# Transposing the values in 32x32 blocks on VectorE and placing the blocks through DRAM

## The chip, the cores and the metric

One core of a Trainium2 chip runs the kernel. It has a matrix engine (TensorE, PE in the profile), a vector engine (VectorE, DVE), an activation engine (ScalarE, ACT), a general engine (GpSimd, POOL) and a sync engine (SyncE, SP), which here issues all DMAs. The metric is the device time of one execution in microseconds; lower is better.

## The reference

The kernel computes one decoder layer on x (1024 tokens by 1024 channels, fp32). After an RMS norm one projection gives eight parts. Three mixers work beside each other: causal pooling, stick-breaking attention with 8 heads of 64 channels, and softmax attention to 256 memory tokens. Every result is multiplied by SiLU of its gate, and an output projection and the residual follow. The part around the change is the stick-breaking attention, cut to what matters:

```python
h = rmsnorm(x, norm_g)
proj = h @ w_in        # pool_v|pool_gate|sb_q|sb_k|sb_v|sb_gate|mem_q|mem_gate
z = (q @ k.T) * Dh**-0.5                       # per head, strictly causal
log_beta, log_1m_beta = log_sigmoid(z), where(mask, log_sigmoid(-z), 0)
cum = cumsum(log_1m_beta, axis=-1)
a = where(mask, exp(log_beta + cum[..., -1:] - cum), 0)
y_sb = (a @ v) * silu(gate)
```

## The kernel before

Matrix products are made in two parts. Each fp32 operand is split into a rounded high part and the rest, its low part, and three products are added up in PSUM (`hh` times `wh`, `hl` times `wh`, `hh` times `wl`).

**Units.** A projection of 128 channels is a `Unit`: two halves of 512 tokens, each of eight steps of three matmuls (L218, L221), and after each half's last step an `evac` function that takes the result out of PSUM. The result stands with the channel on the partition and the token along the row. While a unit starts, the weights of the next one are loaded (L149, on SP), rounded by ACT (L160) and subtracted by POOL (L164).

**The value unit.** For a pair of heads p there is a query, a key, a value and a gate unit. The stick-breaking sum is rewritten by parts, so that the attention multiplies not by v but by the difference between neighbouring tokens. `evac` in `v_unit` makes it: ACT copies the half into `vt` one column to the right (L307), POOL puts the last column of the half before (or a zero, L304) into column 0 (L306), and DVE subtracts (L310). `vt` has one buffer. The attention needs these values with the token on the partition, so a later step, `late`, turns them: PE transposes four blocks of 128x128 into one PSUM bank (L318), ACT rounds them to the high part (L321), and DVE subtracts for the low part (L322). Both go to V, where each head of each block of 128 tokens has 64 columns of high and 64 of low parts.

**Order.** The order of PE's instructions is written by hand. `chain` strings the steps of units together. It puts the first `late` of a value unit at step 13 of that same unit and the second at step 5 of the next unit. `weave` mixes such a string of filling steps into the steps of an attention (first the memory attention, then the four head pairs in turn), by costs that the steps carry (0.43 us for `late`). After the opening stage the order on DVE, ACT, POOL and SP is laid out when the kernel is built, by a planner that takes an instruction once its inputs should be there; on the chip each engine then runs its list in that order. The values of pairs 0 and 1 are made beside the memory attention, those of pairs 2 and 3 beside the attentions of pairs 1 and 2.

Of the kernel before, what the change touches and what calls it, by code (L numbers as in the profile page):

```python
# [8 lines left out]
F32 = mybir.dt.float32  # L9
F32R = mybir.dt.float32r  # L10
AF = mybir.ActivationFunctionType
ALU = mybir.AluOpType
AX = mybir.AxisListType

P = 128
S = 1024
# [4 lines left out]
HD = 64  # L21
# [4 lines left out]
def layer_kernel(  # L26
# [15 lines left out]
    nc = tc.nc  # L42
    const = ctx.enter_context(tc.tile_pool(name="const", bufs=1))
    pool = ctx.enter_context(tc.tile_pool(name="pool", bufs=1))
    psum = ctx.enter_context(tc.tile_pool(name="psum", bufs=1, space=bass.MemoryType.PSUM))

    xv = x[0]
# [5 lines left out]
    def f(ap):  # L53
        return ap.bitcast(F32)
# [3 lines left out]
    def ps(tag, name):  # L58
        return psum.tile([P, 512], F32, tag=tag, name=name, bufs=banks[tag])
# [7 lines left out]
    bufs = {"wr": 1, "wh": 2, "wl": 2, "be": 4}  # L67
# [4 lines left out]
    def slot2(tag, name, dt=F32):  # L72
        return pool.tile([P, 2048], dt, tag=tag, name=name)
# [9 lines left out]
    ident = const.tile([P, P], F32, name="ident")  # L83
# [155 lines left out]
    def chain(units, after=None):  # L239
        steps, rest = [], []  # L240
        for n, u in enumerate(units):
            nxt = units[n + 1] if n + 1 < len(units) else after
            a = list(u.steps)
            if nxt is not None:
                a[0] = (KC, lambda f0=a[0][1], nxt=nxt: (f0(), nxt.weights()))
            if u.late is not None:
                a = a[:13] + u.late(0) + a[13:]
            steps += a[:5] + rest + a[5:]
            rest = u.late(1) if u.late is not None else []
        return steps + rest  # L250

    def lazy(make):
        box = []

        def get():
            if not box:
                box.append(make())
            return box[0]

        return get  # L260
# [35 lines left out]

    def v_unit(e0, name, tag):
        get = lazy(lambda: slot2(tag, f"V_{name}", dt=F32R)[:].rearrange("p (t h c) -> p t h c", t=NT, h=2))
        box = {}

        def evac(th, c, pt):
            vt = pool.tile([P, 513], F32, tag="vt", name=f"vt_{name}_{th}", bufs=1)
            if th == 0:
                nc.gpsimd.memset(vt[:, 0:1], 0.0)  # L304
            else:
                nc.gpsimd.tensor_copy(vt[:, 0:1], vlast[:])  # L306
            nc.scalar.activation(vt[:, 1:513], pt[:], AF.Copy)  # L307
            if th == 0:
                nc.gpsimd.tensor_copy(vlast[:], vt[:, 512:513])
            nc.vector.tensor_tensor(vt[:, 0:512], vt[:, 0:512], pt[:], op=ALU.subtract)  # L310
            box[th] = vt

        def late(th):
            def fn():
                v, vt = get(), box[th]
                tp = ps("tr", f"tv_{name}_{th}")
                for i in range(4):
                    nc.tensor.transpose(tp[:, i * P : (i + 1) * P], vt[:, i * P : (i + 1) * P], ident[:])  # L318
                b = slice(4 * th, 4 * th + 4)
                tpv = tp[:].rearrange("p (b h c) -> p b h c", b=4, h=2)  # L320
                nc.scalar.activation(v[:, b, :, 0:HD], tpv, AF.Copy)  # L321
                nc.vector.tensor_tensor(v[:, b, :, HD:P], tpv, f(v[:, b, :, 0:HD]), op=ALU.subtract)  # L322

            return [(0.43, fn)]

        return get, Unit(e0, name, evac, late)

# [468 lines left out]
    for r in range(2):  # L796
# [7 lines left out]
        for h in range(2):  # L804
            w = 2 << (2 * r + h)
            rows = slice(h * HD, (h + 1) * HD)
# [71 lines left out]
    for p in range(4):  # L878
        b = p % 2
        sb.append(  # L880
            (
                q_unit(512 + p * P, f"q{p}", (f"qa{b}", f"qb{b}"), first=(("av", "tr") if p == 0 else ("pj", "pj")), wtags=(("KA0",) if p == 0 else ("wh", "wl"))),
                k_unit(1024 + p * P, f"k{p}", (f"KA{b}", f"KB{b}")),
                v_unit(1536 + p * P, f"v{p}", f"V{b}"),
                gate_unit(2048 + p * P, f"g{p}", f"G{p}"),
            )
        )
# [45 lines left out]
    for k in range(KD):  # L933
# [5 lines left out]
        if k == 5:  # L939
            mem_ss(0, 1)  # L940
    start.close()
    fill = u_q[0].steps[8:] + chain([u_k[0], u_v[0], u_v[1], u_g[0], u_q[1], u_k[1], u_g[1]], u_q[2])
    cut = 8 + 16 + 17 + 17 + 16
    fill, fill_0 = fill[:cut], fill[cut:]
# [10 lines left out]

    weave(attn(0), fill_0, 4, 1.0)
    weave(attn(1), chain([u_q[2], u_k[2], u_v[2]]+[u_g[2]], u_q[3]), 4, 1.0)
    gp_get = lazy(lambda: slot2("KB0", "gp"))
    gp, u_gp = zip(*[gate_unit(256 + r * P, f"pg{r}", lambda r=r: gp_get()[:, r * 1024 : (r + 1) * 1024]) for r in range(2)])
    gm, u_gm = zip(*[gate_unit(2816 + pr * P, f"mg{pr}", "be", lambda pr=pr: y_mem[pr], (("pj", "pj"), ("tr", "av"))[pr]) for pr in range(2)])  # L960
    u_pv, po = zip(*[pool_parts(r, gp[r]) for r in range(2)])
    weave(attn(2), chain([u_q[3], u_k[3], u_v[3]]+[u_g[3]], u_pv[1]), 4, 1.0)
    fill = chain([u_pv[1], u_gp[1], u_pv[0], u_gp[0]]+[u_gm[0]], u_gm[1])
    for r, at in ((0, 46), (1, 22)):
        for n, st in enumerate(po[r][:-2]):
            fill.insert(at + 2 * n, st)
    at = 70 + len(po[0]) + len(po[1]) - 4
    fill[at:at] = po[0][-2:-1]
    fill[at + 6 : at + 6] = po[0][-1:]
    at = 44 + len(po[1]) - 2  # L970
# [207 lines left out]
```

## Time and profile before

| | |
|---|---|
| time, median of 3 runs (lowest to highest) | 524.44 us (523.58 to 524.48) |
| profiled execution: time, span | 524.41 us, 522.6 us |
| PE busy | 509.8 us (98%) |
| DVE busy | 392.4 us (75%) |
| ACT busy | 289.8 us (55%) |
| POOL busy | 166.4 us (32%) |
| DMA | 37,244 packets, 37.25 MB; 1,990 packets under 512 B |
| granted clock of PE | 1.000 |

The span reaches from the first to the last instruction that the profile records. Busy time counts the records of an engine; records of matmuls that follow each other overlap. A wait is idle time of an engine, put down to the instruction that ended it. The profiler's chain of work that ended last runs over PE for 85% of the span.

### The profile page before, as it was taken

What the parts mean: (1) busy time and instruction counts of PE and PEld (TensorE: products, weight loads), DVE (VectorE), ACT (ScalarE), POOL (GpSimd) and SP (SyncE); (2) the same over time, 40 slices, a digit from 0 to 9 for tenths busy, and PEclk for the clock granted to TensorE, in tenths of its full rate; (3) what the DMA queues carried; (4) which work ended last, traced back from release to release, by engine and by line L of the source; (5) the groups of instructions that cost most, each with busy time, mean ns of one, the idle gap of its engine ahead of it and who ended that gap; (6) DMA issues with size and microseconds to landing.
All of it is one profiled execution on the core that took longest, in us unless ns stands there. A gap on an engine that the chain in (4) does not pass through costs nothing.

```text
span 522.6 us, 7475 instructions
## 1 busy us (share of the span) xinstructions
PE 509.8 (98%) x2724; PEld 429.3 (82%) x2724; DVE 392.4 (75%) x635; ACT 289.8 (55%) x562; POOL 166.4 (32%) x190
## 2 busy tenths in 40 slices
PE   7889999999999999999999999999999999999997
PEld 6678888888888888888888888888788888888886
DVE  4776777777487876877748776748988769999973
ACT  6887657677555654645545655445535539452400
POOL 4480335244212112202201220122436910044890
PEclk9999999999999999999999999999999999999999
DMA  8911021310111131033101122110110525513033
GB/s 298 349 44 41 7 76 43 80 41 0 41 40 42 42 80 41 0 82 80 42 1 40 41 69 54 40 42 7 35 41 0 162 64 180 163 39 135 26 118 124
DMA packets 37244, 37.25 MB, mean 71 GB/s; under 512 B 1990, under 2 KB 26840, under 8 KB 37208
## 3 DMA queue, kind: packets, MB, share of 16 engines
q1 hardware_dynamic: 37208, 36.78, 22.6%
q8 instruction: 21, 0.34, 0.3%
q14 instruction: 15, 0.12, 0.1%
HBM read 28.39 MB, written 4.19 MB: 62 GB/s over the span
## 4 chain that ended last, share of the span: by engine, by line
PE 85%; DVE 6%; ACT 5%; DMA 2%; issue 1%; ACTq 0%; DVEq 0%
PE av L525 8%; PE z L653 7%; PE ta L506 6%; PE u_g L221 6%; PE u_q L221 6%; PE u_v L221 5%; PE u_k L221 5%; PE u_g L218 3%; PE u_mg L221 3%; PE oS L1060 3%; PE u_q L218 3%; PE oS L1062 3%; PE u_pv L221 3%; PE oS L1061 3%; PE u_v L218 3%; PE u_k L218 2%
## 5 line engine op out<-in xcount | busy, mean ns | idle before, releaser
L661 DVE TENSOR_TENSOR_SCAN be<-be,later 128x128 f32<-128x128 f32 (+3 forms) x64 | 92.0, 1452 | 15.8 <-ACT be L657 14.8
L511 ACT ACTIVATE ah<-ta,mone 128x512 fp32r<-128x512 f32 (+1 forms) x80 | 51.6, 645 | 55.7 <-PE ta L506 54.9
L512 DVE SCALAR_TENSOR_TENSOR al<-ta,ah 128x512 fp32r<-128x512 f32 (+1 forms) x80 | 50.6, 632 | 23.3 <-ACT ah L511 22.2
L657 ACT ACTIVATE be<-z 128x128 f32<-128x128 f32 (+3 forms) x96 | 45.6, 490 | 32.4 <-PE z L653 30.8
L506 PE MATMUL ta<-ident,be 128*128 128x128 f32 x288 | 44.9, 273 | 0.0
L506 PEld LDWEIGHTS ta<-ident,be 128*128 128x128 f32 x288 | 34.8, 140 | 7.6 <-DVE be L661 0.6
L525 PEld LDWEIGHTS av<-ah,V_v 128*128 128x128 f32 x160 | 29.7, 188 | 6.7
L525 PE MATMUL av<-al,V_v 128*128 128x256 f32 (+1 forms) x160 | 31.8, 280 | 1.1 <-DVE al L512 1.1
L525 PE MATMUL av<-ah,V_v 128*128 128x256 f32 (+1 forms) x160 | 30.3, 271 | 0.0
L218 PE MATMUL u_g<-hh,wh_g 128*128 128x512 f32 x64 | 27.5, 430 | 0.0
L218 PE MATMUL u_v<-hh,wh_v 128*128 128x512 f32 x64 | 27.3, 426 | 0.0
L164 POOL TENSOR_TENSOR wl_k<-wr_k,wh_k 128x256 fp32r<-128x256 f32 x16 | 12.0, 782 | 45.6 <-ACT wh_k L160 45.6
L218 PE MATMUL u_k<-hh,wh_k 128*128 128x512 f32 x64 | 26.5, 415 | 0.0
L164 POOL TENSOR_TENSOR wl_g<-wr_g,wh_g 128x256 fp32r<-128x256 f32 x16 | 11.3, 742 | 46.4 <-ACT wh_g L160 31.4
L608 POOL TENSOR_SCALAR pe_m<-pe_m,nb_m 128x256 f32<-128x256 f32 x16 | 16.8, 1047 | 29.0 <-DVE nb_m L605 22.4
L1060 PE MATMUL oS<-bs,hh 128*128 128x512 f32 (+1 forms) x68 | 25.9, 381 | 0.0
L1062 PE MATMUL oS<-bs,hl 128*128 128x512 f32 (+1 forms) x68 | 25.8, 379 | 0.0
L1061 PE MATMUL oS<-bs,hh 128*128 128x512 f32 (+1 forms) x68 | 25.6, 377 | 0.0
L221 PE MATMUL u_v<-hl,wh_v 128*128 128x512 f32 x64 | 25.3, 396 | 0.0
L221 PE MATMUL u_g<-hl,wh_g 128*128 128x512 f32 x64 | 25.3, 395 | 0.0
L221 PE MATMUL u_k<-hl,wh_k 128*128 128x512 f32 x64 | 25.3, 395 | 0.0
L221 PE MATMUL u_k<-hh,wl_k 128*128 128x512 f32 x64 | 25.3, 395 | 0.0
(316 smaller groups left out, 1472.1 us busy)
## 6 DMA issues: line engine op xcount, KB each, us to landing
x<-in_x_dram SPq DMA_DIRECT2D x8, 512.0 KB, 6.4
wr_q<-in_w_in_dram SPq DMA_DIRECT2D x4, 512.0 KB, 3.8
wr_k<-in_w_in_dram SPq DMA_DIRECT2D x4, 512.0 KB, 3.6
wr_v<-in_w_in_dram SPq DMA_DIRECT2D x4, 512.0 KB
KA_k<-KA_k SPq DMA_DIRECT2D x8, 256.0 KB, 5.2
KB_k<-KB_k SPq DMA_DIRECT2D x8, 256.0 KB, 4.6
wr_g<-in_w_in_dram SPq DMA_DIRECT2D x4, 512.0 KB, 4.7
xr<-in_x_dram SPq DMA_DIRECT2D x8, 256.0 KB, 3.3
```

The lines of the kernel that those rows point to most:

```text
L218: nc.tensor.matmul(pt[:], wh[:, kc], hh[k][:, c], start=(k == 0), stop=False)
L221: nc.tensor.matmul(pt[:], w[:, kc], h[k][:, c], start=False, stop=(k == KD - 1 and n == 1))
L506: nc.tensor.transpose(tp[:, o : o + P], src, ident[:])
L511: nc.scalar.activation(ah[:, :w], tp[:, :w], AF.Identity, bias=mone[:, 0:1])
L512: nc.vector.scalar_tensor_tensor(al[:, :w], tp[:, :w], -1.0, f(ah[:, :w]), op0=ALU.add, op1=ALU.subtract)
L525: nc.tensor.matmul(av[:, 256 - bw : 256], vs[n], part[:, o : o + bw], start=(first and part is ah and n == 0), stop=(last and part is al a ...
L653: nc.tensor.matmul(zp[:, 0:w], q[h][:, tcol], k[h][:, n, s0 : s0 + w], start=(n == 0), stop=(n == 1))
L657: nc.scalar.activation(be[:, s0 : s0 + w], zp[:, 0:w], AF.Sigmoid, scale=-(HD**-0.5))
L661: nc.vector.tensor_tensor_scan(be[:, rev], be[:, rev], mask, 1.0, op0=ALU.mult, op1=ALU.max)
L1060: nc.tensor.matmul(bk[:, c], xh[:, tcol], wh[:, c], start=(n == 0), stop=False)
L1061: nc.tensor.matmul(bk[:, c], xh[:, tcol], wl[:, c], start=False, stop=False)
L1062: nc.tensor.matmul(bk[:, c], xl[:, tcol], wh[:, c], start=False, stop=(n == 3))
```

## The change

The transposes of the values leave PE. In `evac`, DVE transposes `vt` in place, which turns every 32x32 block within itself and leaves the blocks where they were. Four DMAs, one for each 32 partitions, write the blocks to a DRAM tile `dr` so that each token's row holds its 128 channels. Two DMAs, one for each head, read the rows back into the low part's place in V, token on the partition. `late` is left with two operations: ACT rounds the delivered rows to the high part, and POOL subtracts in place for the low part. `late` carries no PE cost any more, and both calls of it move into the next unit, to steps 5 and 13.

```diff
+    dram = ctx.enter_context(tc.tile_pool(name="dram", bufs=1, space=bass.MemoryType.DRAM))
...
             if u.late is not None:
-                a = a[:13] + u.late(0) + a[13:]
-            steps += a[:5] + rest + a[5:]
-            rest = u.late(1) if u.late is not None else []
-        return steps + rest
+                pass
+            for at, st in rest[::-1]:
+                a[at:at] = st
+            steps += a
+            rest = [(5, u.late(0)), (13, u.late(1))] if u.late is not None else []
+        assert not rest
+        return steps
...
-        box = {}
+        dr = dram.tile([S, P], F32, tag=f"vd_{name}", name=f"vd_{name}")
...
             nc.vector.tensor_tensor(vt[:, 0:512], vt[:, 0:512], pt[:], op=ALU.subtract)
-            box[th] = vt
+
+            nc.vector.transpose(vt[:, 0:512], vt[:, 0:512])
+            rows = slice(512 * th, 512 * th + 512)
+            for a in range(4):
+                q = slice(32 * a, 32 * a + 32)
+                nc.sync.dma_start(
+                    dr[rows, q].rearrange("(b r) c -> r b c", r=32), vt[q, 0:512].rearrange("p (b c) -> p b c", c=32)
+                )
+            for h in range(2):
+                nc.sync.dma_start(
+                    f(get()[:, 4 * th : 4 * th + 4, h, HD:P]),
+                    dr[rows, h * HD : (h + 1) * HD].rearrange("(t p) c -> p t c", p=P),
+                )
 
         def late(th):
             def fn():
-                v, vt = get(), box[th]
-                tp = ps("tr", f"tv_{name}_{th}")
-                for i in range(4):
-                    nc.tensor.transpose(tp[:, i * P : (i + 1) * P], vt[:, i * P : (i + 1) * P], ident[:])
-                b = slice(4 * th, 4 * th + 4)
-                tpv = tp[:].rearrange("p (b h c) -> p b h c", b=4, h=2)
-                nc.scalar.activation(v[:, b, :, 0:HD], tpv, AF.Copy)
-                nc.vector.tensor_tensor(v[:, b, :, HD:P], tpv, f(v[:, b, :, 0:HD]), op=ALU.subtract)
-
-            return [(0.43, fn)]
+                v = get()[:, 4 * th : 4 * th + 4]
+                nc.scalar.activation(v[:, :, :, 0:HD], f(v[:, :, :, HD:P]), AF.Copy)
+                nc.gpsimd.tensor_tensor(v[:, :, :, HD:P], f(v[:, :, :, HD:P]), f(v[:, :, :, 0:HD]), op=ALU.subtract)
+
+            return [(0.0, fn)]
```

## Rows read from the trace of the kernel before

**Rows 1.** The page's busy times: engine, us, share of span, instructions.
```profile
PE 509.8 (98%) x2724; PEld 429.3 (82%) x2724; DVE 392.4 (75%) x635; ACT 289.8 (55%) x562; POOL 166.4 (32%) x190
```

**Rows 2.** Busy time of each engine in stretches; the header names the columns.
```profile
core 0: us, PE busy (x) PEld busy (x) DVE busy (x) ACT busy (x) POOL busy (x), PEclk, DMA share, GB/s
...
66.00:140.00 74.00, 72.74 (x422) 62.16 (x420) 51.95 (x122) 47.91 (x118) 28.79 (x38) 1.00 0.17 47
...
205.00:275.00 70.00, 70.00 (x394) 59.75 (x393) 48.47 (x64) 38.14 (x68) 10.43 (x18) 1.00 0.17 46
275.00:346.00 71.00, 71.00 (x398) 60.77 (x398) 49.79 (x66) 38.35 (x69) 11.23 (x18) 1.00 0.17 45
```

**Rows 3.** Waits of PE, 90 to 116 us: total us, times, longest.
```profile
PE av L525 <- DVE al_m L517: 1.3, 2, 1.1
```

**Rows 4.** Instructions on vt: ns min/median/max, first and last start.
```profile
L318 PE MATMUL tv_v<-ident,vt_v x32: 270/272/273, 102.5 to 331.0; 128*128 128x128 f32 x32
L307 ACT ACTIVATE vt_v<-u_v x8: 588/596/605, 96.6 to 325.9; 128x512 f32<-128x512 f32 x8
L310 DVE TENSOR_TENSOR vt_v<-vt_v,u_v x8: 672/686/691, 97.4 to 326.6; 128x512 f32<-128x512 f32 x8
```

**Rows 5.** Timeline of PE, 250 to 252 us: start us, us, instruction.
```profile
250.31 0.60 PE L318 MATMUL tv_v<-ident,vt_v 128*128 128x128 f32 x4
...
250.99 0.40 PE L221 MATMUL u_v<-hl,wh_v 128*128 128x512 f32 x1
251.22 0.39 PE L221 MATMUL u_v<-hh,wl_v 128*128 128x512 f32 x1
```

**Rows 6.** Timeline of ACT, 99 to 255 us.
```profile
99.58 0.56 ACT L597 ACTIVATE pe_m<-z_m,nb_m,qsc 128x256 f32<-128x256 f32 x1 [1.97 <-DVE nb_m L593]
...
108.15 0.59 ACT L307 ACTIVATE vt_v<-u_v 128x512 f32<-128x512 f32 x1
...
113.50 0.60 ACT L321 ACTIVATE V_v<-tv_v 128x512 fp32r<-128x512 f32 x1
...
117.36 0.60 ACT L307 ACTIVATE vt_v<-u_v 128x512 f32<-128x512 f32 x1
...
123.42 0.60 ACT L321 ACTIVATE V_v<-tv_v 128x512 fp32r<-128x512 f32 x1
...
127.43 0.59 ACT L307 ACTIVATE vt_v<-u_v 128x512 f32<-128x512 f32 x1
...
128.45 1.06 ACT L160 ACTIVATE wh_q<-wr_q 128x1024 fp32r<-128x1024 f32 x1
...
244.45 0.60 ACT L307 ACTIVATE vt_v<-u_v 128x512 f32<-128x512 f32 x1
...
254.32 0.59 ACT L307 ACTIVATE vt_v<-u_v 128x512 f32<-128x512 f32 x1
```

**Rows 7.** Timeline of DVE, 109 to 246 us.
```profile
109.91 0.67 DVE L310 TENSOR_TENSOR vt_v<-vt_v,u_v 128x512 f32<-128x512 f32 x1
...
118.06 0.69 DVE L310 TENSOR_TENSOR vt_v<-vt_v,u_v 128x512 f32<-128x512 f32 x1
...
245.15 0.69 DVE L310 TENSOR_TENSOR vt_v<-vt_v,u_v 128x512 f32<-128x512 f32 x1
```

**Rows 8.** Groups by line and shape: count, then busy us, mean ns, idle before.
```profile
L661 DVE TENSOR_TENSOR_SCAN be<-be,later 128x512 f32<-128x512 f32 x8 | 9.7, 1212 | 0.9 <-ACT be L657 0.7
L1036 POOL TENSOR_TENSOR b_V<-b_V,b_V 128x512 f32<-128x512 f32 x4 | 6.0, 1510 | 0.0
L322 DVE TENSOR_TENSOR V_v<-tv_v,V_v 128x512 fp32r<-128x512 f32 x8 | 5.5, 682 | 0.9 <-ACT V_v L321 0.9
```

**Rows 9.** DMA issues: count, KB each, median us from issue to landing.
```profile
KA_k<-KA_k SPq DMA_DIRECT2D x8, 256.0 KB, 5.2
...
out_dram<-xr SPq DMA_DIRECT2D x8, 256.0 KB, 3.1
...
pw<-in_pool_w_dram SPq DMA_DIRECT2D x4, 16.0 KB, 1.9
```

**Rows 10.** One line's issues on SP: ns min/median/max, first and last start.
```profile
L293 SPq DMA_DIRECT2D KA_k<-KA_k x8: 596/600/687, 80.6 to 311.3; - x8
```

**Rows 11.** Timeline of SP at 110 us.
```profile
110.00 0.37 SPq L149 DMA_DIRECT2D wr_q<-in_w_in_dram  x1
```

## The prediction

> **What bounds the kernel now.** I read the page's busy times first: TensorE (PE) is busy in 98% of the span [rows 1]. A busy PE is not always at its own pace, so the second view is busy time by stage [rows 2]. Four projections of values (v0 to v3) lie in three stages. v0 and v1 are made between 66 and 140 us, beside the memory attention, and v2 and v3 in the second and third stick-breaking stages. In 205 to 275 us PE is busy 70.00 of 70.00 us, DVE 48.47 and ACT 38.14; 275 to 346, the stage of v3, looks the same. In 66 to 140 PE is busy 72.74 of 74.00 us and DVE and ACT about two thirds. The granted clock is 1.00 in both, the 2.4 GHz level. The third view, PE's waits, shows in the part of the memory stage where v0 is made just two, for the low half of a transposed probability on DVE, 1.3 us in sum [rows 3]. So in the stages that the change touches PE sets the end, and work taken off PE is worth its full length as long as no other engine comes late.
>
> **What is removed.** 32 PE transposes leave: eight groups (four v, two halves) of four [rows 4]. The records' 272 ns overlap, so I take the pace from the timeline [rows 5]: the group starts at 250.31, the second matmul behind it at 250.99; one 512-column matmul lies between, at the pace of 0.23 us that the next start, 251.22, shows. 0.68 - 0.23 = 0.45 us. Eight times that is 3.6 us; I take 3.5, since a group that follows another transpose starts with less delay. In the attention stages (four groups) PE never waited, so 1.75 us is gained in full; in the memory stage (four groups) as long as ACT and DVE follow.
>
> **What is added on DVE, ACT and POOL.** DVE loses eight subtractions out of PSUM, 0.68 us each [rows 8], and gets eight transposes of 128x512 fp32 in place. No row shows a DVE transpose: it costs between nothing and the 1.21 us of a scan over the same shape [rows 8]. I take the 0.68 us of the tensor-tensor that streams as many columns, so DVE's total is unchanged (ends -5.5 and +4.2 us over the kernel, with over 20 us of DVE idle per stage to hide either [rows 2]). The Trainium skill, page "VectorE: DVE Perf Modes", section "The three transpose paths", gives 311 ns for a 128x128 bf16 transpose; four of these would be, as an estimate from that page, 1.24 us, some 4.5 us more DVE time in all and still inside the idle time. ACT's copy of the high half stays at about 0.6 us but reads the delivered rows in place of PSUM. The subtraction goes to POOL, 1.51 us by the nearest row [rows 8], eight times 12 us. In 66 to 140 us POOL is busy 28.79 us of 74, in the attention stages under 12 of 70 and 71 [rows 2], so this fits; half of every memory probability is scaled on POOL, though, and one caught behind a subtraction is 1.5 us late. A v is first read in the stage after the one that makes it, so the subtraction's own latency costs nothing.
>
> **The way through DRAM.** Each half now issues six DMAs from SP: four writes (32 partitions, pieces of 128 B) that wait for the DVE transpose, and two reads (pieces of 256 B) that wait for the writes. An issue takes up to 0.60 us [rows 10]. To landing: the smallest transfer 1.9 us, the write to DRAM of 256 KB 3.1 us, the slowest kind (SBUF to SBUF) 5.2 us [rows 9]. I take 3.1, the only one of the three that writes to DRAM. The out trip, from the end of the subtraction at L310 until the buffer is free, is then 0.68 + 4 x 0.60 + 3.1 = 6.2 us; its ends are 0 + 4 x 0.37 + 1.9 = 3.4 (0.37 is the issue of rows 11) and 1.21 + 2.4 + 5.2 = 8.8 us. The trip back adds 2 x 0.60 + 3.1 = 4.3 us.
>
> Two things wait for these. First, vt has one buffer: the next half's ACT copy (L307) and POOL's tiny column copy ahead of it used to wait for PE's transposes and now wait for the writes. ACT copies start at 96.6, 108.15, 117.36, 127.43, and 244.45, 254.32 [rows 4, 6]; v3 repeats v2's pattern. The subtraction ends at 110.58, 118.75, 245.84 [rows 7]. With 0.25 us for POOL's column copy (0.15 for the memset of a new v), the room left for the out trip is 117.21 - 110.58 = 6.6 us, 127.18 - 118.75 = 8.4 us and 254.07 - 245.84 = 8.2 us, the last twice; the first reuse, with the widest gap (11.5 us), has over 9. At 6.2 us all five fit, the tightest by 0.4 us. At 8.8 us three reuses miss by 0.4 to 0.6 us and one by 2.2. Behind a blocked ACT stand the exponentials and probability copies that feed PE. ACT has idle gaps of up to 2 us at such places (before the start at 99.58 [rows 6]); I count 1.2 us of a block as covered, an estimate between no gap and that one. The upper end costs about 1 us then.
>
> Second, the late copies. The first half of a v is copied where the second was before, the second where the next v's first was. For v0: first half 98.1 + 6.2 + 4.3 = 108.6 us, wanted at 113.50; second half 110.6 + 10.5 = 121.1, wanted at 123.42 [rows 6]. They fit by 4.9 and 2.3 us. At both upper ends (8.8 + 6.4 = 15.2) the first is in time by 0.2 us and the second 2.4 us late, less 1.2 covered.
>
> On SP the writes and reads stand among the weight loads; a load behind a read that waits for its writes is late by up to about 6 us. The load wr_q, sent at 110.00, is first used at 128.45 [rows 11, 6], 18 us later and more than three of the slowest landings: cover enough. If that cover were gone, PE would stop at a new unit, up to 6 us each time.
>
> **Sum.** The profiled execution took 524.41 us (span 522.6 and 1.8 around it), the median is 524.44, so they are one number. 524.4 - 3.5 = 520.9. For what I cannot see, mostly ACT and POOL caught in order behind an arrival, I add 0.7 us, one covered-less block of the tightest reuse and one delayed POOL scaling: 521.6 us.
>
> **Rivals.**
> - *Only half is paid.* In the memory stage PE already waits for DVE's al_m (1.3 us [rows 3]); with less on PE this wait grows by what was removed, and 1.75 us of the 3.5 is lost: 524.4 - 1.75 = 522.7 us. For it: two waits of that kind, and POOL work of 1.5 us put among the scalings. Against: 72.74 of 74 us busy.
> - *Handed back.* The landings are at their upper end, and four late copies (2.4 - 1.2 us each would be 4.8, half of them hidden at the seam to the next stage) and the tight reuse (1 us) take 2.5 to 4 us: 523.4 to 524.9, centre 524.3 us. For it: the reuse that fits by 0.4 us. Against: it needs both ends at once.
> - *Slower: the single vt buffer decides.* If an out trip takes 11 us, the rooms of 6.6, 8.2, 8.2, 8.4 are missed by 4.4, 2.8, 2.8 and 2.6 us, less 1.2 covered each: 3.2 + 1.6 + 1.6 + 1.4 = 7.8 us; 520.9 + 7.8 = 528.7 us. It decides from a trip of 10 us on (2.2 + 0.6 + 0.6 + 0.4 = 3.8 us, the gain). For it: 2,048 pieces per half, and no write of such small pieces in the trace. Against: the issues take 2.4 us in which the first pieces already drain. A rule of the Trainium skill speaks for it ("DMA: Bandwidth & Descriptors", section "Specifications"): transfers under 512 B are read, modified and written. If every write landed at twice 3.1 us by that rule, the trip would be an estimated 9.3 us and the time 520.9 + (9.3 - 6.6 - 1.2) = 522.4; no run here shows it.
> - *Does it do what it says?* All PE transposes of v are gone from the code, so PE's part is certain; that case has no chance of its own.
>
> **How the numbers follow.** The forecast has 0.47, its own range 520.4 to 522.4. Half paid has 0.15 (522.0 to 523.3). Handed back has 0.19; slower 0.19. A measurement of this kernel tells about 0.2%, 1.05 us. Faster by more is below 523.4: 0.47 + 0.15 = 0.62. Within 0.2%: 0.19; slower 0.19. The range runs from 520.3, everything gained and a little of PE's waits with it, to 525.8, which leaves out the larger part of the slower case.
>
> **What would show it.** Right: no record of tv in the trace, PE's busy time down by about 3.5 us in the three stages, ACT's copy into vt waiting less than a microsecond for DMA, writes landing in about 3 us, the span near 519.8. Half paid: PE's waits for al_m between 66 and 140 us up by about 1.8 us. Wrong: ACT at L307 or at the late copies waiting for DMA for several microseconds, POOL's scalings late behind them, and PE idle in stages where it had none; or weight copies on ACT waiting for loads that SP sent late.

## The result, and the profile after

| | before | after |
|---|---|---|
| time, median (lowest to highest) | 524.22 us (523.58 to 524.48, 4 runs) | 520.71 us (520.45 to 520.84, 4 runs) |
| profiled execution: time, span | 524.41, 522.6 us | 520.78, 519.0 us |
| granted clock of PE | 1.000 | 1.000 |

The ratio is 0.9934, 95% interval 0.9919 to 0.9949: 3.5 us faster. The forecast was 521.6 us.

The page's busy times of the changed kernel, to set against [rows 1]:

```profile
PE 506.7 (98%) x2692; PEld 426.1 (82%) x2692; DVE 391.2 (75%) x635; ACT 289.1 (56%) x562; POOL 177.8 (34%) x198
```

PE lost 3.1 us and the 32 transposes, DVE stayed level, POOL gained 11.4 us. By stage, with the columns of [rows 2]:

```profile
66.00:140.00 74.00, 72.54 (x415) 61.79 (x414) 53.03 (x124) 48.51 (x121) 32.50 (x41) 1.00 0.32 75
205.00:275.00 70.00, 70.00 (x390) 59.67 (x389) 49.99 (x66) 38.52 (x70) 14.37 (x21) 1.00 0.24 57
275.00:346.00 71.00, 71.00 (x395) 60.72 (x394) 50.37 (x67) 38.52 (x70) 14.31 (x20) 1.00 0.25 61
```

PE is as full as before in every stretch, so busy shares cannot show the gain. What shows it is when recurring events come. The timeline of SP before, the send of each pair's key halves (first halves) and a weight load after the last value:

```profile
171.30 0.60 SPq L293 DMA_DIRECT2D KA_k<-KA_k  x1
...
228.64 0.60 SPq L293 DMA_DIRECT2D KA_k<-KA_k  x1
...
300.22 0.60 SPq L293 DMA_DIRECT2D KA_k<-KA_k  x1
...
348.05 0.37 SPq L149 DMA_DIRECT2D wr_pv<-in_w_in_dram  x1
```

and after:

```profile
169.41 0.60 SPq L297 DMA_DIRECT2D KA_k<-KA_k  x1
...
226.75 0.60 SPq L297 DMA_DIRECT2D KA_k<-KA_k  x1
...
297.43 0.60 SPq L297 DMA_DIRECT2D KA_k<-KA_k  x1
...
344.41 0.37 SPq L150 DMA_DIRECT2D wr_pv<-in_w_in_dram  x1
```

The lead is 1.89 us after the memory stage (v0 and v1, four groups), still 1.89 at 227 us (no value in between), 2.79 behind v2 and 3.64 behind v3. A lead of 0.21 us stood before the first changed instruction (SP's load wr_k left at 39.43 before, at 39.22 after), so the change brought 1.68, 0.90 and 0.85 us, 3.43 in all: two groups bring 0.84 to 0.90 us everywhere, 0.43 us each. The span ends 3.6 us earlier: nothing is given back later.

The new operations, the instructions on vt and V (ns min/median/max, first and last start, shapes):

```profile
L320 SPq DMA_DIRECT2D vd_v<-vt_v x32: 320/498/767, 100.3 to 328.4; - x32
L316 DVE STREAM_TRANSPOSE vt_v<-vt_v x8: 686/711/712, 99.5 to 326.1; 128x512 f32<-128x512 f32 x8
```

```profile
L324 SPq DMA_DIRECT2D V_v<-vd_v x16: 376/377/519, 102.7 to 331.0; - x16
L332 ACT ACTIVATE V_v<-V_v x8: 620/628/642, 110.4 to 337.1; 128x512 fp32r<-128x512 f32 x8
L333 POOL TENSOR_TENSOR V_v<-V_v x8: 1282/1290/1292, 111.9 to 337.8; 128x512 fp32r<-128x512 f32 x8
```

and their DMAs (count, KB each, median us from issue to landing):

```profile
vd_v<-vt_v SPq DMA_DIRECT2D x32, 64.0 KB, 2.0
V_v<-vd_v SPq DMA_DIRECT2D x16, 128.0 KB, 2.2
```

The DVE transpose took 0.71 us, a write of 512 pieces of 128 B landed in 2.0 us. The median hides a spread: the writes sent from 112.39 us on, beside a weight load, took 3.7 us to land. The waits of PE in 66 to 140 us, total, times, longest; in 205 to 346 us it has none, before and after:

```profile
PE z_m L598 <- ACT pe_m L608: 1.1, 1, 1.1
PE av L536 <- DVE al_m L528: 0.4, 1, 0.4
```

PE stood for 1.5 us there in place of 1.3. On ACT no copy into vt waits for a DMA; POOL's clearing of column 0 does once, 1.2 us. Two of the copies of delivered rows do, 2.76 and 2.84 us, one each in the stages of v2 and v3. The first, on ACT's timeline, and what SP did before it:

```profile
258.89 0.63 ACT L332 ACTIVATE V_v<-V_v 128x512 fp32r<-128x512 f32 x1 [2.76 <-DMA V_v<-vd_v]
```

```profile
251.79 0.38 SPq L324 DMA_DIRECT2D V_v<-vd_v  x1
254.53 0.39 SPq L150 DMA_DIRECT2D wr_k<-in_w_in_dram  x1
255.03 0.52 SPq L324 DMA_DIRECT2D V_v<-vd_v  x1
```

The second read of that half stood behind a weight load that had to wait for its room: 255.03 in place of 252.2. ACT stood for it, and PE did not notice.

### The profile page after: what moved, and what is told of

The parts are those of the page before. It is cut to its first block, busy times and chain, and to the rows that moved or that the text cites. A ratio compares the mean times of both kernels' runs of the same rounds, so it can differ in the third digit from the quotient of the medians.

```text
span 519.0 us, 7552 instructions
## 1 busy us (share of the span) xinstructions
PE 506.7 (98%) x2692; PEld 426.1 (82%) x2692; DVE 391.2 (75%) x635; ACT 289.1 (56%) x562; POOL 177.8 (34%) x198
## 4 chain that ended last, share of the span: by engine, by line
PE 88%; ACT 5%; DVE 4%; DMA 1%; issue 1%; SPq 0%; ACTq 0%
PE av L536 8%; PE z L664 7%; PE ta L517 6%; PE u_v L222 6%; PE u_q L222 6%; PE u_g L222 5%; PE u_k L222 5%; PE u_q L219 3%; PE u_v L219 3%; PE u_mg L222 3%; PE oS L1071 3%; PE oS L1073 3%; PE u_pv L222 3%; PE oS L1072 3%; PE u_g L219 3%; PE u_k L219 3%
## 5 line engine op out<-in xcount | busy, mean ns | idle before, releaser
L608 ACT ACTIVATE pe_m<-z_m,nb_m,qsc 128x256 f32<-128x256 f32 x32 | 17.8, 560 | 13.6 <-DVE nb_m L604 13.4
L536 PEld LDWEIGHTS av<-al,V_v 128*128 128x128 f32 x160 | 24.1, 189 | 1.4 <-DVE al L523 1.3
```

Source lines behind the costliest of these rows:

```text
L536: nc.tensor.matmul(av[:, 256 - bw : 256], vs[n], part[:, o : o + bw], start=(first and part is ah and n == 0), stop=(last and part is al a ...
```

## The experiments

Ratios are to the kernel before on the same chip; between the runs here its median was 523.99 to 524.22 us. Theory A: PE's own time is the gain, and the DRAM way is hidden. Its rival at first: the gain comes from somewhere else (the order, DVE's work moved to POOL), or the DRAM way already takes part of a larger gain back.

**PE's work put back.** Beside the changed path, `late` issues four PE transposes per half again; their result is not used.

```diff
+                tp = ps("tr", f"tv_{name}_{th}")
+                for i in range(4):
+                    nc.tensor.transpose(tp[:, i * P : (i + 1) * P], ident[:], ident[:])
...
-            return [(0.0, fn)]
+            return [(0.43, fn)]
```

> The changed kernel with eight groups of four PE transposes put back beside it (of the identity, into a PSUM bank that nothing reads, at the places of the late steps, with their old cost of 0.43 us). Theory (the gain is PE's own time): all of it goes again, ratio to the kernel before 0.9995 to 1.0015, and the stages of v0 and v1 end about 1.8 us later than in the changed kernel, those of v2 and v3 0.9 us later each. Rival 1 (the gain comes from the new order of the late steps, or from work that left ACT, DVE or the PSUM banks' drains, not from PE): the ratio stays near 0.9935. Rival 2 (half and half): 0.996 to 0.998.

Measured: 524.27 us, ratio 1.0002 [0.9993, 1.001]. The whole gain is gone. By stage less was lost than expected: the marks of SP's timeline came 1.05 us later than in the changed kernel behind v0 and v1, 2.18 behind v2 and 3.28 behind v3, where 1.8, 2.7 and 3.6 were expected. Of what is missing behind v0 and v1, 0.36 us is a lead that stood before the change acts (wr_k left at 38.86 us), and 0.4 is waiting: PE stood for 1.1 us in the memory stage, in the changed kernel for 1.5.

With the cost of 0.43 us `weave` mixes PE's own instructions differently, so the order of PE goes back with its work. What separates the two are the waits: in 205 to 346 us PE has none before, after or here, so there no order of it can gain or lose.

**Transposes free of cost.** The kernel before, with ACT and DVE reading vt directly.

```diff
-                tp = ps("tr", f"tv_{name}_{th}")
-                for i in range(4):
-                    nc.tensor.transpose(tp[:, i * P : (i + 1) * P], vt[:, i * P : (i + 1) * P], ident[:])
...
-                tpv = tp[:].rearrange("p (b h c) -> p b h c", b=4, h=2)
+                tpv = vt[:, 0:512].rearrange("p (b h c) -> p b h c", b=4, h=2)
...
-            return [(0.43, fn)]
+            return [(0.0, fn)]
```

> The kernel before with the values' transposes left out: the late steps split the untransposed vt straight into V (ACT copy and DVE subtraction, same shapes), at the old places, at a PE cost of 0. The values are not turned, so it shows what transposes that cost nothing would bring. Theory (the way through DRAM is hidden entirely): ratio 0.9925 to 0.994, the same as the changed kernel within 0.1%. Rival (the way through DRAM costs something that the gain covers up, for instance ACT's waits of 2.8 us for the delivered rows): 0.990 to 0.9915, faster than the changed kernel by 1 us or more.

Measured: 521.01 us, 0.994 [0.9927, 0.9952]. Transposes that cost nothing bring no more than those through DRAM: the way is hidden, as far as these intervals (some 0.7 us to either side) can tell. Theory A stands; how much room it has was the next question.

**A longer way: writes doubled.** The first four of eight writes go to a DRAM tile that nobody reads. The next kernel issues each four times.

```diff
-            for a in range(4):
+            for a, to in [(a, d) for d in waste + [dr] for a in range(4)]:
...
-                    dr[rows, q].rearrange("(b r) c -> r b c", r=32), vt[q, 0:512].rearrange("p (b c) -> p b c", c=32)
+                    to[rows, q].rearrange("(b r) c -> r b c", r=32), vt[q, 0:512].rearrange("p (b c) -> p b c", c=32)
```

> The changed kernel with each of the four writes issued twice, first all four into a DRAM tile that nothing reads. SP issues 4 more DMAs of 0.5 us per half, so the time from the subtraction until vt is free grows from about 4.9 to about 6.9 us where the DVE transpose follows at once. Theory (the single vt buffer has room; ACT's blocks of up to 2.8 us do not reach PE): ratio 0.993 to 0.9945. Rival (by the price in the prediction, room of 6.6 us and 1.2 us of cover): 0.9935 to 0.9955, not yet to be told apart; it is the low step of a scale with the run of four times.

> The changed kernel with each write issued four times, three of them into DRAM tiles that nothing reads: 16 issues of 0.5 us, so vt is free some 11 us after the subtraction. By the prediction's slower rival (rooms of 6.6, 8.2, 8.2 and 8.4 us, 1.2 us of cover each): 7 to 8 us lost, ratio 1.006 to 1.010, with ACT at its copy into vt or POOL at the column waiting several microseconds for DMA. Theory now (a wait of ACT costs PE less than the price assumed, since blocks of 2.8 us passed unseen): part of it, 2 to 5 us, ratio 0.997 to 1.003. If vt's release didn't matter at all: 0.993 to 0.9945.

Measured: 534.55 us, 1.0204 [1.0186, 1.0223], and 556.83 us, 1.0618 [1.0602, 1.0634]. Both expectations failed by far. In the first, PE waits 2.6 and 5.1 us in the memory stage for DVE's subtraction on vt. It frees the PSUM bank of that half, and the halves take turns on two banks: the next half but one stands until then.

**Other lengthenings.** Four copies from DRAM to DRAM between writes and reads, which delay the delivery but not the release of vt; and two extra writes in place of four.

```diff
+            for a in range(4):
+                q = slice(32 * a, 32 * a + 32)
+                nc.sync.dma_start(waste[rows, q].rearrange("(b r) c -> r b c", r=32), dr[rows, q].rearrange("(b r) c -> r b c", r=32))
             for h in range(2):
```

> The changed kernel with four more DMAs per half that copy the rows just written from DRAM to DRAM (same pieces, into a tile that nothing reads), between the writes and the reads: SP issues as many DMAs as with doubled writes and the DMA engines move as many bytes, but vt is free as soon as the four writes have landed. Theory (doubled writes cost 14 us because vt is given back late): ratio 0.993 to 0.997. Rival (SP's issue time, or the load of small pieces on the DMA engines, is what costs): 1.01 or more, as with doubled writes.

> The changed kernel with two more writes per half (half the dose of the doubled writes, 1 us more until vt is free), ahead of the four. Theory (a threshold: the order laid out at build time moves the next half's copy behind the next round of attention work as soon as vt is free later than it reckons): either nothing, 0.993 to 0.9945, or most of the 14 us, above 1.01. Rival (a cost in proportion to the delay): half of it, 1.005 to 1.009.

Measured: 538.25 us, 1.0272 [1.0258, 1.0286], and 525.62 us, 1.0026 [1.0017, 1.0035]. The theory of the first failed, and the second lies in none of the three ranges. So vt's release isn't the only way to lose. With the copies, PE's longest wait has another cause; its timeline, and SP's ahead of it:

```profile
150.83 0.80 PE L219 MATMUL u_q<-hh,wh_q 128*128 128x512 f32 x1 [8.25 <-ACT wh_q L161]
```

```profile
139.68 1.96 SPq L321 DMA_DIRECT2D vd_v<-vt_v  x4
141.74 2.55 SPq L326 DMA_DIRECT2D vw_v<-vd_v  x4
144.34 1.16 SPq L328 DMA_DIRECT2D V_v<-vd_v  x2
145.55 0.51 SPq L150 DMA_DIRECT2D wr_q<-in_w_in_dram  x1
```

The load wr_q, sent at 111.92 us in the changed kernel, was laid behind the value's DMAs and left at 145.55. In the kernel with doubled writes, ACT's copy into vt moved from 108.86 to 116.21 us, although the doubled writes were issued by 104.4 and landed some 2 us later. Both point to the order that the planner lays for the longer way, theory B; the rival, C, is that the chip itself holds vt or the rows too long.

**First try at B against C.** Edges that put the refill of vt ahead of all attention work traced behind it, with the writes doubled and, as control, without.

```diff
+            with ExitStack() as order:
+                for i in first:
+                    order.enter_context(tc.issue_after(i))
                 s.fn()
...
+            first[:] = [getattr(i, "ins", i) for i in (col, cp, sub)]
```

> The doubled writes again, with order edges that put the refill of vt (ACT's copy, POOL's column, DVE's subtraction) ahead of all attention work traced after it on the same engine; no DMA and no buffer differs. Theory (the writes themselves land in time; what costs is that the planner, reckoning with a later release, put the refill 5 to 6 ACT instructions further back, so that PE waits for the PSUM bank which the refill reads): ratio 0.993 to 0.998. Rival (vt really is held that long, so ACT now stands still at the copy for several microseconds): 1.010 to 1.025.

> The changed kernel with the same order edges and no additional writes. Theory: ACT's list changes by two or three places in v1 to v3 only; ratio 0.992 to 0.994, the same as the changed kernel. Rival (the edges themselves cost or save): outside of that.

Measured: 541.92 us, 1.0333 [1.0312, 1.0354], and the control 531.43 us, 1.0156 [1.0135, 1.0177]; the expectation for the control failed. The edges alone cost 10.7 us: in the control engines stand at the refill (DVE's subtraction waits 10.0 us for POOL's small copy, 4 times) in place of doing attention work. The pair says nothing on B or C, only that a refill can also come too early.

**The order held.** The lists of ACT, DVE, POOL and SP were taken from the changed kernel and laid as chains of order-only edges over the same instructions in three kernels: writes doubled, writes four times, copies between. Extra DMAs stand in SP's list directly ahead of the DMA that they delay. The fourth kernel is the changed one, nothing added, with the lists of the kernel with doubled writes.

```diff
+    for row in ORDER:
+        last = None
+        for k in row:
+            for i in before.get(seq[k].name, []) + [seq[k]]:
+                if last is not None:
+                    tc.add_manual_dep(i, last.name, after)
+                last = i
```

> The kernel with every write issued twice (ratio 1.0204 with the order that was planned for it), but with the lists of ACT, DVE, POOL, SP and PE held in the order of the changed kernel; the four extra writes of a half stand in SP's list directly ahead of the four real ones. If the re-laid order made the loss: between 0.993 and 0.996 of the kernel before, since the out trip grows by four issues of 0.50 us (2 us) and the changed kernel's vt copies on ACT waited for no DMA at all. If the longer hold of the buffer on the chip made it, whatever the order: 1.015 to 1.022 again. Half way, 1.003 to 1.010, would need both.

> The changed kernel's own instructions, with nothing added, in the order that was planned for the kernel with doubled writes (without the extra writes). If order alone makes the loss: 1.013 to 1.021. If it takes the chip's longer hold: 0.993 to 0.996. In between, the order costs what the ratio shows and the doubled writes on the chip the rest.

> Four copies from DRAM to DRAM between the writes and the reads of each half (ratio 1.0272 with its own order, where a weight load had slipped behind them), in the order of the changed kernel. They delay the delivery by about 4 us (four issues and a landing) and hold vt only as far as SP's list does. If order made the loss: 0.993 to 0.998; the late copies on ACT then wait up to 6.8 us in place of 2.8, of which a part may show on PE. If a late delivery itself costs that much: 1.02 or more.

> Every write issued four times, in the order of the changed kernel. The out trip is then 0.71 + 16 x 0.50 + 2.0 = 10.7 us, the 11 us of the prediction's slower case. By the prediction's price for it (rooms of 6.6, 8.4, 8.2, 8.2 and some 9 us, 1.2 us of a block covered) 520.7 + 2.9 + 1.1 + 1.3 + 1.3 + 0.5 = 527.8 us, ratio 1.006. If 2.8 us of a block are covered, as ACT's late copies of the changed kernel show: 520.7 + 1.3 = 522.0, ratio 0.996. If the hold on the chip is what cost so much with its own order (1.0618): 1.04 or more.

| kernel | own order | order of the changed kernel |
|---|---|---|
| writes doubled | 1.0204 | 520.98 us, 0.9937 [0.992, 0.9954] |
| copies between | 1.0272 | 521.43 us, 0.9946 [0.9932, 0.9961] |
| writes four times | 1.0618 | 541.95 us, 1.0341 [1.0326, 1.0357] |
| changed kernel, in the order for doubled writes | 535.36 us, 1.0212 [1.0196, 1.0227] | 0.9934 |

B is shown for the first two: the same DMAs, in the old lists, cost 0.3 and 0.7 us in place of 13.8 and 17.5, and the other list without any extra DMA costs the whole 14.6. Between the two lists only 83 of ACT's 519 places differ, 42 of DVE's 635, 33 of POOL's 196 and 15 of SP's 160. PE's waits in the fourth kernel and in the one with doubled writes in its own order are the same to 0.1 us, so where it is lost can be read in the fourth. ACT's timeline there:

```profile
110.63 0.57 ACT L610 ACTIVATE pe_m<-z_m,nb_m,qsc 128x256 f32<-128x256 f32 x1 [1.24 <-PE av L538]
...
114.71 0.56 ACT L610 ACTIVATE pe_m<-z_m,nb_m,qsc 128x256 f32<-128x256 f32 x1 [1.99 <-DVE nb_m L606]
...
116.28 0.60 ACT L313 ACTIVATE vt_v<-u_v 128x512 f32<-128x512 f32 x1
...
126.23 1.06 ACT L161 ACTIVATE wh_q<-wr_q 128x1024 fp32r<-128x1024 f32 x1 [0.66 <-PE u_v L222]
...
128.76 0.60 ACT L313 ACTIVATE vt_v<-u_v 128x512 f32<-128x512 f32 x1
```

ACT idles 1.24 and 1.99 us for probability work while vt has been free since about 104 us, and copies into it at 116.28; the next copy stands behind the rounding of weights, at 128.76 (changed kernel: 119.45). The subtraction behind that copy then stands 1.52 us more for POOL's clearing of column 0, which comes after a weight subtraction of 2.86 us in POOL's list:

```profile
131.22 0.69 DVE L316 TENSOR_TENSOR vt_v<-vt_v,u_v 128x512 f32<-128x512 f32 x1 [1.52 <-POOL vt_v L310]
```

PE's timeline pays for both, and its granted clock with it (columns: us, PE busy, clock, DMA share, GB/s):

```profile
117.82 0.50 PE L219 MATMUL u_v<-hh,wh_v 128*128 128x512 f32 x1 [2.61 <-DVE vt_v L316]
...
126.27 0.60 PE L519 MATMUL ta_m<-ident,pe_m 128*128 128x128 f32 x4
131.96 0.80 PE L219 MATMUL u_g<-hh,wh_g 128*128 128x512 f32 x1 [5.09 <-DVE vt_v L316]
132.55 0.63 PE L222 MATMUL u_g<-hl,wh_g 128*128 128x512 f32 x1
132.97 0.63 PE L222 MATMUL u_g<-hh,wl_g 128*128 128x512 f32 x1
```

```profile
124.00:128.00 4.00, 2.87 (x19) 1.00 0.00 0
128.00:132.00 4.00, 0.04 (x1) 0.73 0.07 17
132.00:136.00 4.00, 4.00 (x14) 0.50 0.97 214
136.00:140.00 4.00, 4.00 (x22) 0.92 0.29 66
```

By the marks 10.5 of the 13.8 us between this trace and the changed kernel's arise in the memory stage. Most of the rest are two waits of PE, 1.4 us each, for DVE's product at a gate in the stages of v2 and v3 (205 to 346 us; the changed kernel has none there):

```profile
PE u_g L219 <- DVE g_g L347: 2.8, 2, 1.4
```

**Four writes: here C is true for the larger part.** With the order held this kernel still loses 21.2 us against the changed one, of 36.1 in its own order; 1.0341 lies above both prices of the expectation and below its 1.04. Its waits on ACT in 90 to 140 us:

```profile
ACT vt_v L314 <- DMA vd_v<-vt_v: 9.1, 3, 5.5
ACT V_v L341 <- DMA V_v<-vd_v: 0.6, 1, 0.6
```

In 140 to 175 and 205 to 400 us come 4.5 and 3.6 us more for vt, and 6.9, 5.0 and 4.7 us for delivered rows (six waits): 17.2 us for each of the two, 34.4 us in all. For PE the 5.52 us block of ACT, ended at 126.43 us, reads so:

```profile
124.05 0.60 PE L526 MATMUL ta_m<-ident,pe_m 128*128 128x128 f32 x4
127.86 0.50 PE L219 MATMUL u_g<-hh,wh_g 128*128 128x512 f32 x1 [3.21 <-DVE vt_v L317]
...
132.31 0.63 PE L222 MATMUL u_g<-hl,wh_g 128*128 128x512 f32 x1
132.74 0.63 PE L222 MATMUL u_g<-hh,wl_g 128*128 128x512 f32 x1
```

Two waits (3.21 and 0.89 us behind it) and then work at 0.43 us per matmul until 135.7 us, at a granted clock of 0.61 and 0.54, some 3 us more: this block cost more than its own length. Not every one did: the 34.4 us in all cost 21.2.

## Why the prediction was right, and where it was not

**The bound and what leaves PE: right.** 3.5 us for eight groups of 0.45, paid in all stages; the marks give 1.68 + 0.90 + 0.85 = 3.43. The two experiments on PE's work bracket it: all of the gain goes when it is put back, and none is left to win when it is free. The sign that PE's busy time would fall by 3.5 us in the three stages didn't come, since PE stays as full; over the whole span it fell by 3.1. *Only half paid* failed at its sign: PE's wait for al_m, 1.3 us in [rows 3], didn't grow but fell to 0.4, and with the new wait of 1.1 for ACT's probability copy PE stood 0.2 us longer, not 1.75.

**What comes to DVE, ACT and POOL: right.** 0.71 us against the 0.68 taken for the transpose; 1.29 against 1.51 for POOL's subtraction. The estimate from the Trainium skill, page "VectorE: DVE Perf Modes", section "The three transpose paths" (four times 311 ns, 1.24 us), lies 0.53 us above this fp32 measurement; nothing hung on it.

**The out trip: its terms off, the fit partly luck.** The issue was 0.50 us in the median, not 0.60 ([rows 10] has a longest of 0.687, and one write here took 0.77), the landing 2.0, not 3.1. For the first half of v0, whose subtraction started at 98.8, that gives 0.71 + 4 x 0.50 + 2.0 = 4.7 us. But the sum left out waiting on DVE and behind other transfers. The planner put a scan of 2.29 us between v2's subtraction (ended 244.44) and its transpose (246.56); the first read, which needs only two of the four writes, left 7.3 us after the subtraction, at 251.79, over the 6.2 forecast for all four. ACT's copy at 253.85 still found vt free. In the second half of v0 the writes left right behind the load wr_q (timeline of the changed kernel):

```profile
109.55 0.69 DVE L314 TENSOR_TENSOR vt_v<-vt_v,u_v 128x512 f32<-128x512 f32 x1 [0.15 <-issue]
...
111.92 0.37 SPq L150 DMA_DIRECT2D wr_q<-in_w_in_dram  x1
...
112.39 2.63 SPq L320 DMA_DIRECT2D vd_v<-vt_v  x4
...
116.77 1.80 SPq L324 DMA_DIRECT2D V_v<-vd_v  x2
...
119.45 0.60 ACT L311 ACTIVATE vt_v<-u_v 128x512 f32<-128x512 f32 x1
```

The second of the two reads waits for the last write; it took 0.38 us and ended the pair at 118.57, so it left at 118.19, and this trip took some 7.9 us. The prediction gave that reuse, the tightest, a room of 6.6 us: by that room it would have missed by 1.3. It fitted because the planner laid ACT's copy later, at 119.45 in place of 117.36, behind one more pair of probability copies, and PE did not wait for it. That the lists move with the change was no part of the prediction; here it helped, in the experiments it cost.

*A rule against the change.* The write of [rows 9] moves 256 KB in 3.1 us, each of these 64 KB in 2.0 us in the median and 3.7 in the slowest half, and doubling them in the held order cost 0.3 us in all. The Trainium skill, page "DMA: Bandwidth & Descriptors", section "Specifications", has transfers under 512 B read, modified and written; here a landing at twice the forecast 3.1 us, which the rule's rival wanted, does not occur. No run here compares pieces of 128 B with larger ones of the same bytes, so the rule itself is not tested.

**The trip back and SP: covered, but by more than I gave.** I worried about a weight load behind a read; what came was a read behind a weight load, and 2.8 us blocks on ACT in two stages. (With the copies between, in the lists laid for them, the worry came true: the load behind the reads stopped PE for 8.25 us.) At the 1.2 us of cover that I counted they would have cost 1.6 us each; they cost PE nothing. The margin of 0.7 us was not needed: 520.9 was the better sum (520.71 measured).

**The slower rival: priced far too low.** It gave 528.7 us for a trip of 11 us. The kernel with four writes in the held order has that trip (subtraction ended about 99.4, ACT's copy released at 110.37) and takes 541.95. Of the step "the rooms of 6.6, 8.2, 8.2, 8.4 are missed by 4.4, 2.8, 2.8 and 2.6 us, less 1.2 covered each" the misses are near (ACT waited 5.5, 4.5, 3.6 and 2.1 us, and 1.5 at the first reuse); it left out that the rows come late as well, another 17.2 us of ACT, and that the block of 5.5 us was not covered in part but cost more than itself, by the clock. And it took the lists for given. The planner lays them anew for every length of the way, and there the loss began far below a trip of 10 us: two more issues per half cost 4.9 us (525.62 against 520.71), four cost 13.8 at a trip of some 7 us. For the four the held order shows the cause; for the two, copies into vt at 111.86 and 125.33 us in place of 108.86 and 119.45 point to it, but no run held their order.

## What to carry to other kernels

Work taken off the engine that bounds every stage is paid at its pace, and a detour that is hidden costs nothing: test both ends, by putting the work back and by making it free. Where a planner lays the lists, a change in the length of a path changes the order of everything near it; hold the order before the chip is blamed for what a longer path costs. Slack read from one order holds in that order only: the room of 6.6 us in the old lists was some 9 us in the new ones.

## What had not been expected of the hardware

After a wait of 5.09 us PE came back at half pace: the granted clock was 0.50 in 132 to 136 us of the kernel in the other order (1.2 GHz, 0.43 us from one 512-column matmul to the next, where 0.23 is usual), and 1.00 again from 140 us on. With the copies between, 148 to 152 us behind the 8.25 us wait show 0.50 too. In the kernel with four writes the pace fell behind two waits, 3.21 and 0.89 us, with three matmuls between them. The 2.61 us wait at 117.82 left the clock at 1.00. So a long wait on PE can cost more than its length: 4 us at nearly half pace here lose some 2 us, the 7 us behind the block in the kernel with four writes some 3.

What stays open: which single place of the other order decides. The two late copies into vt, and behind the second POOL's late clearing of column 0, stand ahead of PE's two waits, but no run moved only them.
